# Two-layer hybrid decoder trunk on one core: gate/up columns in another order, the FFN's input at 64-byte multiples, and narrow passes at the start of two stretches

## The chip, the cores and the metric

The kernel runs on one core of a Trainium2 chip. The metric is device time in microseconds (us) of one execution. TensorE (PE in the profile, with PEld for its weight loads) multiplies, VectorE (DVE) and ScalarE (ACT) do the elementwise work, SyncE (SP) issues the transfers, GpSimd (POOL) does next to nothing here.

## The reference

Two layers over 256 positions and 1024 features. In each layer a SwiGLU feed-forward block (FFN), a mixer (low-rank attention beside a short convolution) and a second FFN; each starts from an RMS norm whose output is scaled and shifted by values computed from a conditioning vector.

```python
for l in range(DEPTH):
    mod = jnp.split(c_act @ w_ada[l] + b_ada[l], N_MOD, axis=-1)
    h = modulate(rms_norm(x, ffn1_norm[l]), mod[0], mod[1])
    x = x + FFN_RESIDUAL * (1 + mod[2])[:, None, :] * swiglu(h, ffn1_w_gu[l], ffn1_w_down[l])
    h = modulate(rms_norm(x, mix_norm[l]), mod[3], mod[4])
    y = hybrid_mixer(h, cos, sin, w_in[l], ...)
    x = x + (1 + mod[5])[:, None, :] * y
    h = modulate(rms_norm(x, ffn2_norm[l]), mod[6], mod[7])
    x = x + FFN_RESIDUAL * (1 + mod[8])[:, None, :] * swiglu(h, ffn2_w_gu[l], ffn2_w_down[l])
return rms_norm(x, final_norm)
# swiglu(h, w_gu, w_down): g, u = split(h @ w_gu); (silu(g) * u) @ w_down     with D_FF = 2816
```

## The kernel before

Features lie on the 128 partitions: `x` is 8 rows of 128 features by 256 positions, and so is the FFN's input `u`. Every weight is read from memory once, in chunks of 16 tiles of 128 by 128 (1 MB).

**Precision by parts.** A float32 factor is split into a rounded high part and the remainder. ACT makes `hi` of a chunk and DVE makes `lo` from `raw` and `hi` (L262 and L265), two halves of eight tiles each; ACT and DVE do the same for the input, into uH (L355) and uL (L359, L361). A weight tile then takes the products hi·uH, hi·uL and lo·uH. In `mm3` these are three passes of 256 columns. In `mm3w` ("wide") one pass of 512 columns takes uL and uH together, since they lie side by side, and a second pass of 256 columns adds lo·uH. With `split`, `mm3w` issues the 512 columns as two passes of 256 ("narrow"). Each pass loads its weights anew.

**The FFN.** There are four, here named by layer and place: (0,0), (0,2), (1,0), (1,2). Each has 22 gate/up chunks: chunk j holds the eight tiles (over the eight input rows k) of 128 gate columns and the eight of 128 up columns, in the order k = 0 gate, k = 0 up, k = 1 gate, and so on. The output of a chunk goes through ACT and DVE (Silu, product, split) into the tile `a`, a row of 2048 bytes for each chunk. Then come 11 down chunks: for each of eight output blocks m, 22 tiles, each fed by one row of `a`.

The first four chunks of (0,2), (1,0) and (1,2) ("late", `LATE = 4`) run on an unnormed input, in narrow passes with two more columns for the shift, while the norm is still being computed; their results are corrected afterwards. During the fourth one ACT and DVE write the normed and modulated input into `u`, row by row (the L355 and L359 instructions that read `qh` and `e`). From the fifth chunk on (j = 4) the passes are wide and read `u`. FFN (0,0) runs its gate/up in narrow passes throughout.

**The layout of u.** One tile with rows of 2·256 + 2 = 514 float32, that is 2056 bytes, which is 32 times 64 plus 8: row k begins 8k bytes past a multiple of 64. The first 256 columns are uL, then uH, then the shift's two columns.

**Order.** PE, DVE and ACT each work through one queue in order. The order in it is made by a list scheduler from priorities: `due` sets them, from a clock that each matmul advances by its columns, with leads for loads and slack for evacuations. The mixer's order on PE and SP is written by hand, and so is SP's throughout: for each chunk the load of `raw` and, behind it, the loads of `ada` (w_ada, from which DVE computes the modulation at L189). `raw`, `hi` and `lo` have three buffers each, `ada` four.

The split passes before: one whole chunk, (1,0) j = 21, and in the down part the first 4 tiles of (0,2) and the first 22 of (1,2):

```python
mm3w(pt[:, h, :], w, 2 * k + h, u[:, k, :2 * S], uH[:, k, :S], k == 0, k == KD - 1, (l, sub, j) == (1, 0, NJ - 1))
...
mm3w(ps, w, t % 16, aB[k], aH[k], k == 0, k == NJ - 1, t < (0 if sub == 0 else 22 if l else 4))
```

Of the kernel before, what the change touches and what calls it, by code (L numbers as in the profile page):

```python
# [12 lines left out]
F32R = mybir.dt.float32r  # L13
# [5 lines left out]
P = 128  # L19
L = 2  # L20
D = 1024
S = 256
KD = D // P
FF = 2816
NJ = FF // P
# [6 lines left out]
CH = 16 * P  # L32
# [3 lines left out]
LATE = 4  # L36
# [2 lines left out]
ENGS = {'p': mybir.EngineType.PE, 's': mybir.EngineType.SP, 'v': mybir.EngineType.DVE, 'a': mybir.EngineType.Activation}  # L39
MAN = 'sp'  # L40
SM_ACT = 2
ORDER = ("K K Q Q K X K Q Q P P P L c c c P c N Z V v q0 q1 s0 q2 c c c c t0 s1 a0 q3 c c c t1 c a1 s2 s3 c c c c t2 d d a2 t3 d a3 "
         "d d n d w d d A A A w m A A w A A A B B B B B B B B").split()
WIN = dict(K=0, Q=1, P=2, c=3, d=7)
# [75 lines left out]
def trunk(ctx: ExitStack, tc, x_d, c_d, pos_d, small_d, cst_d, ada_d, gu1_d, dn1_d, win_d, up_d, wo_d, gu2_d, dn2_d, out_d):  # L120
    nc = tc.nc
    one = ctx.enter_context(tc.tile_pool(name="one", bufs=1))
# [7 lines left out]
    def nm(s):  # L130
        uid[0] += 1
        return f"{s}_{uid[0]}"
# [7 lines left out]
    def work(shape, tag, bufs=2, dt=F32):  # L140
        return wk.tile(shape, dt, tag=tag, name=nm(tag), bufs=bufs)
# [4 lines left out]
    x = one.tile([P, KD, S], F32, name="x")  # L146
    cb = one.tile([P, D], F32, name="cb")
    small = one.tile([P, SM_W], F32, name="small")
    cst = one.tile([P, C_W], F32, name="cst")
    u = one.tile([P, KD, 2 * S + 2], F32R, name="u")  # L150
    uL, uH = u[:, :, 0:S], u[:, :, S:]
    ones = one.tile([P, P], F32, name="ones")
    tq = one.tile([P, S], F32, name="tq")
    tk = one.tile([P, S], F32, name="tk")
# [135 lines left out]
    def mm3(dst, w, t, aH, aL, first, last, ext=0):  # L290
        hi, lo = w[-2:]
        n = S + ext
        wh = hi[:, t * P:(t + 1) * P]
        wl = lo[:, t * P:(t + 1) * P]
        mm(dst[:, :n], wh, aH[:, :n], start=first, stop=False, skip_group_check=True)
        mm(dst[:, :S], wh, aL, start=False, stop=False, skip_group_check=True)
        mm(dst[:, :n], wl, aH[:, :n], start=False, stop=last, skip_group_check=True)

    def mm3w(dst, w, t, both, up, first, last, split=False):


        hi, lo = w[-2:]
        wh = hi[:, t * P:(t + 1) * P]
        wl = lo[:, t * P:(t + 1) * P]
        if split:
            mm(dst[:, :S], wh, both[:, :S], start=first, stop=False, skip_group_check=True)
            mm(dst[:, S:], wh, both[:, S:], start=False, stop=False, skip_group_check=True)
        else:
            mm(dst, wh, both, start=first, stop=False, skip_group_check=True)
        mm(dst[:, :S], wl, up, start=False, stop=last, skip_group_check=True)  # L310
# [43 lines left out]
    def hi_of(dH, src, scale=1.0):  # L354
        nc.scalar.activation(dH, src, AF.Copy, scale=scale)  # L355

    def lo_of(dL, dH, src, scale=None):
        if scale is None:
            nc.vector.tensor_tensor(dL, src, f32(dH), ALU.subtract)  # L359
        else:  # L360
            nc.vector.scalar_tensor_tensor(dL, src, scale, f32(dH), ALU.mult, ALU.subtract)  # L361

    class Pre:


        def __init__(self, l, sub):
            self.l, self.sub = l, sub
            self.gs = work([P, 8], "gs", 2)
            self.stat = Stat(D)

# [7 lines left out]
            return g  # L378

        def shifts(self):  # L380
            hcol = uH[:, :, S:S + 1].squeeze(2)
            lcol = uH[:, :, S + 1:S + 2].squeeze(2)
            sh = self.shift(0, KD)
            nc.scalar.activation(hcol, sh, AF.Copy)
            nc.vector.tensor_tensor(lcol, sh, f32(hcol), ALU.subtract)

        def put(self, k, add=True):
            g = self.scale(k)
            hi_of(uH[:, k, :S], x[:, k, :], g)
            lo_of(uL[:, k, :], uH[:, k, :S], x[:, k, :], g)  # L390
            if add:
                self.stat.add(x[:, k, :])

# [15 lines left out]
    def ffn(l, sub, pre, nxt, first=False):  # L409
        def evac(j, pg, pu, r):  # L410
# [20 lines left out]
            if j == NJ - 1:  # L431
                warm(sg[:, 0:1], AF.Abs_reciprocal_sqrt)

        j0 = 0
        if first:
            r = work([P, S], "r", 1)
# [12 lines left out]
            with tc.manual_schedule():  # L449
# [18 lines left out]
                for k in range(KD):  # L468
# [6 lines left out]
                    w, top, rest = load(True) if k else w0  # L475
# [22 lines left out]
        aL, aH = ([ab[k // (NJ // 2)][:, k % (NJ // 2), q, :] for k in range(NJ)] for q in range(2))  # L498
        aB = [ab[k // (NJ // 2)][:, k % (NJ // 2)].rearrange("p a s -> p (a s)") for k in range(NJ)]
        for j in range(j0):  # L500
            z = slice((j % 2) * S, (j % 2 + 1) * S)
            due(GU_SLACK + 1000 * j)
            evac(j, pts[j // 2][:, 0, z], pts[j // 2][:, 1, z], None)
        for j in range(j0, NJ):
            w = chunk()
            if first and j == 10:
                due(ROPE_SLACK)
                nc.sync.dma_start(cst, cst_d)
                nc.sync.dma_start(pi, pos_d)
                rope()  # L510
            late = not first and j < LATE
            wide = not first and not late
            pt = ps_tile()
            for k in range(KD):
                for h in range(2):
                    if wide:
                        mm3w(pt[:, h, :], w, 2 * k + h, u[:, k, :2 * S], uH[:, k, :S], k == 0, k == KD - 1, (l, sub, j) == (1, 0, NJ - 1))
                    else:
                        mm3(pt[:, h, :], w, 2 * k + h, uH[:, k, :], uL[:, k, :], k == 0, k == KD - 1, 2 if late else 0)
            if late and j == 0:  # L520
                r = work([P, S], "r", 1)
                pre.stat.rstd(r, then=AF.Silu)
                due(0)
                hs = [work([P, 2, S], "qh", 2) for _ in range(2)]
                he = [work([P, 2, 384], "e", 2).rearrange("p a b -> p (a b)") for _ in range(2)]
                hf = [hs[k // 2][:, k % 2, :] if k < 4 else he[k // 2 - 2][:, k % 2 * S:(k % 2 + 1) * S] for k in range(KD)]
                for k in range(KD):
                    xr = work([P, S], "nt", 2)
                    nc.vector.tensor_tensor(xr, x[:, k, :], r, ALU.mult)  # L529
                    nc.scalar.activation(hf[k], xr, AF.Identity, scale=pre.gs[:, k:k + 1], bias=pre.shift(k))  # L530
            if late and j == LATE - 1:
                due(-URGENT)
                for k in range(KD):
                    hi_of(uH[:, k, :S], hf[k])
                    lo_of(uL[:, k, :], uH[:, k, :S], hf[k])
            due(GU_SLACK if j < NJ - 3 else 0)
            if late:
                evac(j, pt, None, r)
            elif wide:
                evac(j, pt, None, None)  # L540
            else:
                evac(j, pt[:, 0, :S], pt[:, 1, :S], None)
        if nxt is None:
            y = [wk.tile([P, 4, S], F32, tag="ada", name=nm("y"), bufs=4) for _ in range(2)]
        for t in range(KD * NJ):
            m, k = divmod(t, NJ)
            if t % 16 == 0:
                w = chunk()
            if k == 0:
                ps = ps_tile()[:, 0, :]  # L550
            if m < KD - 1:
                mm3w(ps, w, t % 16, aB[k], aH[k], k == 0, k == NJ - 1, t < (0 if sub == 0 else 22 if l else 4))
            else:
                mm3(ps, w, t % 16, aH[k], aL[k], k == 0, k == NJ - 1)
            if k == NJ - 1:
                due(DN_SLACK if m < KD - 1 else -URGENT)
                residual(ps, m, l, sub, 0.5, m < KD - 1)
                if nxt is None:
                    if m == KD - 1:
                        psf = ps_tile()[:, 0, :S]  # L560
                        fin.sums(psf, True, False)
                        due(-URGENT)
                        fin.acc = None
                    fin.add(x[:, m, :])
                    nc.scalar.activation(y[m // 4][:, m % 4, :], x[:, m, :], AF.Copy, scale=small[:, L * SM_L + m:L * SM_L + m + 1])
                    if m == KD - 1:
                        last_norm(psf, y)
                else:
                    nxt.put(m)
                    if m == 5:  # L570
                        nxt.shifts()

    def mixer(l, pre, nxt):
        mf = one.tile([P, NJ, S], F32, tag="aH", name=nm("mf"))
        mr = one.tile([P, NJ, S], F32R, tag="aL", name=nm("mr"))
        ckv, cq, conv, V, K = mf[:, 0:2], mf[:, 2:5], mf[:, 5:9], mf[:, 9:13], mf[:, 13:21]
# [317 lines left out]
    pre = Pre(0, 0)  # L894
# [18 lines left out]
def _layout(a):  # L913
    g = {}
# [17 lines left out]
    for f in (1, 2):  # L932
        t = _tiles(a[f"ffn{f}_w_gu"]).reshape(L, KD, 2, NJ, P, P)
        w = t.transpose(0, 3, 4, 1, 2, 5).reshape(L, NJ, P, CH)
        if f == 1:
            head = w[0, :8].reshape(8, P, 8, 2, P).transpose(2, 1, 0, 3, 4).reshape(1, 8, P, CH)
            w = np.concatenate([np.concatenate([head, w[:1, 8:]], axis=1), w[1:]], axis=0)
        g[f"gu{f}"] = np.ascontiguousarray(w)
        t = _tiles(a[f"ffn{f}_w_down"]).transpose(0, 2, 1, 3, 4).reshape(L, 11, 16, P, P)
        g[f"dn{f}"] = np.ascontiguousarray(t.transpose(0, 1, 3, 2, 4).reshape(L, 11, P, CH))  # L940
    w = a["w_in"]
# [41 lines left out]
```

## Time and profile before

| | |
|---|---|
| three runs | 993.0, 990.76, 993.14 us, median 993.0 |
| profiled execution | 993.62 us, of which 990.9 us are the span of its instructions |
| granted TensorE clock | 0.998 |
| DVE, ACT busy | 852.4 us (86%), 580.3 us (59%) |
| read from memory | 248.59 MB, 252 GB/s over the span |

The page gives for each engine how long it was busy, then the chain of work that ended last, then groups of instructions. The records of matmuls overlap, because they are pipelined: a pass of 512 columns is recorded with 0.39 us and the next one starts some 0.23 us after it began. How fast the passes follow each other is therefore read from starts, or from the number of passes in a stretch, and not from their mean duration. Which stretch is which, in us from the start of the span: FFN (0,0) to 205, mixer to 311, (0,2) gate/up to 438 and down to 500, (1,0) gate/up from there to 627 and down to 689, mixer to 794, (1,2) gate/up to 919 and down to the end.

### The profile page before, as it was taken

How to read it: one execution, taken by the hardware profiler on the slowest of the kernel's cores; microseconds unless marked ns; L12 is line 12 of the kernel's file. 1: busy time of each engine (PE TensorE's matmuls, PEld its weight loads, DVE VectorE, ACT ScalarE, POOL GpSimd, SP SyncE). 2: the span in 40 equal slices, each digit the busy share in tenths (PEclk: the TensorE clock that was granted, in tenths of full speed). 3: DMA queues.
4: the chain of work that ended last, by engine and by line, in shares of the span. 5: the costliest groups of instructions: out<-in, count | busy, mean ns of one | idle time of the engine just before them, and what ended most of it. 6: DMA issues, size and time to landing. Idle time of an engine off the chain costs nothing.

```text
span 990.9 us, 16909 instructions
## 1 busy us (share of the span) xinstructions
PE 973.8 (98%) x6602; PEld 897.2 (91%) x6602; DVE 852.4 (86%) x1598; ACT 580.3 (59%) x1010; POOL 8.0 (1%) x27
## 2 busy tenths in 40 slices
PE   8999999999999999999999999999999999999996
PEld 7999998899999988888898888889999998888985
DVE  5999999999989999888879988888899999866653
ACT  4474544468758756554466555544687676556551
POOL 0000020000000000000000000000000000000000
PEclk9999999999999999999999999999999999999999
DMA  9999898873746688777867877876455467555531
GB/s 348 382 361 349 321 327 322 298 306 137 263 161 239 216 323 327 272 267 271 292 217 294 291 282 260 304 273 247 149 211 195 149 240 294 210 184 198 176 123 42
DMA packets 47007, 250.78 MB, mean 253 GB/s; under 512 B 5504, under 2 KB 5824, under 8 KB 26576
## 3 DMA queue, kind: packets, MB, share of 16 engines
q1 hardware_dynamic: 46224, 248.81, 68.5%
q8 instruction: 51, 0.84, 0.3%
q10 hardware_dynamic: 288, 0.65, 0.2%
q0 software_dynamic: 416, 0.25, 0.1%
q14 instruction: 28, 0.23, 0.1%
HBM read 248.59 MB, written 1.10 MB: 252 GB/s over the span
## 4 chain that ended last, share of the span: by engine, by line
PE 88%; DVE 6%; DMA 3%; ACT 1%; issue 1%; DVEq 0%; SPq 0%; ACTq 0%
PE ps L287 87%; DVE lo L265 2%; DMA raw<-in_gu 2%; DMA ada<-in_ada 1%; DVE ada L189 1%; PE ps L736 1%; ACT hi L262 1%; DMA cb<-in_c 0%; DVE acc L326 0%; DVE u L361 0%; DVE x L399 0%; DVE nt L599 0%; DVE mr L359 0%; DVE nt L529 0%; DVE rs_a L347 0%
## 5 line engine op out<-in xcount | busy, mean ns | idle before, releaser
L287 PE MATMUL ps<-u,hi 128*128 128x256 f32 (+2 forms) x2480 | 596.6, 322 | 2.6 <-DVE u L359 1.1
L287 PE MATMUL ps<-u,lo 128*128 128x256 f32 (+1 forms) x1664 | 469.1, 282 | 1.1 <-DVE lo L265 1.1
L287 PEld LDWEIGHTS ps<-u,hi 128*128 128x128 f32 x2480 | 413.1, 189 | 40.9 <-ACT hi L262 1.3
L265 DVE TENSOR_TENSOR lo<-raw,hi 128x1024 fp32r<-128x1024 f32 (+2 forms) x384 | 394.5, 1045 | 38.3 <-ACT hi L262 38.0
L262 ACT ACTIVATE hi<-raw 128x1024 fp32r<-128x1024 f32 (+2 forms) x384 | 336.9, 911 | 91.3 <-PE ps L287 37.3
L287 PEld LDWEIGHTS ps<-u,lo 128*128 128x128 f32 x1664 | 314.7, 189 | 1.6 <-DVE lo L265 1.6
L287 PE MATMUL ps<-a,hi 128*128 128x512 f32 (+1 forms) x818 | 247.9, 364 | 0.0
L189 DVE CUSTOM_DVE_ANT_0 ada<-ada,cb,small 128x1024 f32<-128x1024 f32 x144 | 183.0, 1279 | 32.7 <-DMA ada<-in_ada 32.6
L287 PE MATMUL ps<-a,lo 128*128 128x256 f32 x704 | 197.8, 281 | 0.0
L287 PEld LDWEIGHTS ps<-a,hi 128*128 128x128 f32 x818 | 145.9, 188 | 26.2 <-DVE a L359 0.2
L287 PEld LDWEIGHTS ps<-a,lo 128*128 128x128 f32 x704 | 133.2, 189 | 0.0
L355 ACT ACTIVATE a<-cc 128x256 fp32r<-128x256 f32 x88 | 36.3, 415 | 63.0 <-DVE cc L418 54.0
L287 PE MATMUL ps<-mr,hi 128*128 128x256 f32 x384 | 71.3, 286 | 0.7 <-ACT mr L355 0.5
L355 ACT ACTIVATE u<-x,gs 128x256 fp32r<-128x256 f32 x40 | 19.9, 506 | 80.4 <-DVE x L399 80.1
L287 PEld LDWEIGHTS ps<-mr,hi 128*128 128x128 f32 x384 | 60.3, 191 | 2.2 <-ACT mr L355 0.9
L287 PE MATMUL ps<-mr,lo 128*128 128x256 f32 x192 | 54.7, 285 | 0.0
L399 DVE SCALAR_TENSOR_TENSOR x<-ps,gate,x 128x256 f32<-128x256 f32 x76 | 36.0, 480 | 17.7 <-PE ps L287 17.1
L417 ACT ACTIVATE cc<-g 128x256 f32<-128x256 f32 x54 | 22.5, 417 | 45.3 <-DVE g L416 45.2
L359 DVE TENSOR_TENSOR a<-cc,a 128x256 fp32r<-128x256 f32 x88 | 36.7, 420 | 12.6 <-ACT a L355 12.5
L287 PEld LDWEIGHTS ps<-mr,lo 128*128 128x128 f32 x192 | 36.7, 191 | 0.8 <-DVE lo L265 0.8
L416 DVE TENSOR_TENSOR g<-ps,g 128x512 f32<-128x512 f32 x54 | 36.9, 684 | 0.4 <-ACT g L415 0.4
L415 ACT ACTIVATE g<-ps 128x512 f32<-128x512 f32 x54 | 31.3, 579 | 7.7 <-PE ps L287 7.7
(121 smaller groups left out, 566.1 us busy)
## 6 DMA issues: line engine op xcount, KB each, us to landing
raw<-in_gu SPq DMA_DIRECT2D x87, 1024.0 KB, 5.8
ada<-in_ada SPq DMA_DIRECT2D x144, 512.0 KB, 6.2
raw<-in_dn SPq DMA_DIRECT2D x44, 1024.0 KB, 5.2
raw<-in_win SPq DMA_DIRECT2D x18, 1024.0 KB, 5.0
raw<-in_wo SPq DMA_DIRECT2D x8, 1024.0 KB, 4.9
raw<-in_up SPq DMA_DIRECT2D x2, 1024.0 KB, 5.5
raw<-in_up SPq DMA_DIRECT2D x2, 768.0 KB, 5.0
raw<-in_up SPq DMA_DIRECT2D x4, 384.0 KB, 3.2
```

The source lines that it names most:

```text
L189: nc.vector.tensor_tensor_reduce(out=a, in0=a, in1=cb, scale=1.0, scalar=sm(l, t), op0=ALU.mult, op1=ALU.add, accum_out=mods[l][:, t:t + 1])
L262: nc.scalar.activation(hi[:, zs[q]], raw[:, zs[q]], AF.Copy)
L265: nc.vector.tensor_tensor(lo[:, zs[q]], raw[:, zs[q]], f32(hi[:, zs[q]]), ALU.subtract)
L287: nc.tensor.matmul(dst, a, b, **kw)
L355: nc.scalar.activation(dH, src, AF.Copy, scale=scale)
L359: nc.vector.tensor_tensor(dL, src, f32(dH), ALU.subtract)
L399: nc.vector.scalar_tensor_tensor(x[:, m, :], s, g, x[:, m, :], ALU.mult, ALU.add)
L415: nc.scalar.activation(t2, pg[:, :, :S], AF.Copy)
L416: nc.vector.tensor_tensor(t2, pg[:, :, S:], t2, ALU.add)
L417: nc.scalar.activation(sg, t2[:, 0, :], AF.Silu)
L736: nc.tensor.transpose(ps[:, e, z], d["e"][:, e, z], ident)
```

## The change

- From the fifth chunk on, in (0,2), (1,0) and (1,2), a chunk holds its eight gate tiles first and its eight up tiles after them, and the loop runs so (`h` outside, `k` inside). The weights are laid out accordingly beforehand, so the 16 tiles of a chunk are still read front to back.
- `u` becomes a flat tile `uf` with two views on the same bytes: `u_near` with the old rows of 2056 bytes, for (0,0) and the mixers, and `u_far` with rows of 528 float32 or 2112 bytes, 33 times 64, for (0,2), (1,0) and (1,2).
- Narrow passes: the whole chunk j = 4 in these three FFNs (before: j = 21 of (1,0)), and the whole first output block of the down part, 22 tiles, in these three (before: 4, 0 and 22 tiles).

```diff
+U_NEAR, U_FAR, U_COLS = 0, 0, 2 * S + 16
...
-    u = one.tile([P, KD, 2 * S + 2], F32R, name="u")
-    uL, uH = u[:, :, 0:S], u[:, :, S:]
+    uf = one.tile([P, U_FAR + KD * U_COLS], F32R, name="u")
+    u_far = uf[:, U_FAR:].rearrange("p (k c) -> p k c", c=U_COLS)[:, :, :2 * S + 2]
+    u_near = uf[:, U_NEAR:U_NEAR + KD * (2 * S + 2)].rearrange("p (k c) -> p k c", c=2 * S + 2)
...
+            self.u = u_near if sub == 1 or (l, sub) == (0, 0) else u_far
+            self.uL, self.uH = self.u[:, :, 0:S], self.u[:, :, S:]
...
-            for k in range(KD):
+            for h in range(2 * wide):
+                for k in range(KD):
+                    mm3w(pt[:, h, :], w, h * KD + k, u[:, k, :2 * S], uH[:, k, :S], k == 0, k == KD - 1, j == LATE)
+            for k in range(KD * (not wide)):
                 for h in range(2):
-                    if wide:
-                        mm3w(pt[:, h, :], w, 2 * k + h, u[:, k, :2 * S], uH[:, k, :S], k == 0, k == KD - 1, (l, sub, j) == (1, 0, NJ - 1))
-                    else:
-                        mm3(pt[:, h, :], w, 2 * k + h, uH[:, k, :], uL[:, k, :], k == 0, k == KD - 1, 2 if late else 0)
+                    mm3(pt[:, h, :], w, 2 * k + h, uH[:, k, :], uL[:, k, :], k == 0, k == KD - 1, 2 if late else 0)
...
-                mm3w(ps, w, t % 16, aB[k], aH[k], k == 0, k == NJ - 1, t < (0 if sub == 0 else 22 if l else 4))
+                mm3w(ps, w, t % 16, aB[k], aH[k], k == 0, k == NJ - 1, m == 0 and (l, sub) != (0, 0))
...
+        for q in range(2 - f, L):
+            z = w[q, LATE:].reshape(NJ - LATE, P, KD, 2, P)
+            w[q, LATE:] = z.swapaxes(2, 3).reshape(NJ - LATE, P, CH)
```

The same place on PE, before: the last pass of the late chunks of FFN (1,0) and the first tiles of j = 4, with what each pass waits for (hi and lo are the weights, ps the accumulator).

```order
L287 MATMUL ps_5827<-u,lo_5818 128x258
L287 MATMUL ps_5912<-u,hi_5902 128x512 [waits DVE_49]
L287 MATMUL ps_5912<-u,lo_5903 128x256
L287 MATMUL ps_5912<-u,hi_5902 128x512
L287 MATMUL ps_5912<-u,lo_5903 128x256
L287 MATMUL ps_5912<-u,hi_5902 128x512 [waits DVE_49]
L287 MATMUL ps_5912<-u,lo_5903 128x256
L287 MATMUL ps_5912<-u,hi_5902 128x512
L287 MATMUL ps_5912<-u,lo_5903 128x256
L287 MATMUL ps_5912<-u,hi_5902 128x512 [waits DVE_49]
```

And there after the change:

```order
L289 MATMUL ps_5861<-u,lo_5852 128x258
L289 MATMUL ps_5946<-u,hi_5936 128x256 [waits DVE_49]
L289 MATMUL ps_5946<-u,hi_5936 128x256 [waits Activation_49]
L289 MATMUL ps_5946<-u,lo_5937 128x256
L289 MATMUL ps_5946<-u,hi_5936 128x256 [waits DVE_49]
L289 MATMUL ps_5946<-u,hi_5936 128x256 [waits Activation_49]
L289 MATMUL ps_5946<-u,lo_5937 128x256
L289 MATMUL ps_5946<-u,hi_5936 128x256 [waits DVE_49]
L289 MATMUL ps_5946<-u,hi_5936 128x256 [waits Activation_49]
L289 MATMUL ps_5946<-u,lo_5937 128x256
```

Before, every second tile waits for a new row of u (two tiles share a row); now every tile does, until the eight rows are through, and a tile has three passes.

The other side of these waits, DVE in the same place, before: it writes the low part of the eight rows (u from qh, then from e; the first row's instruction stands just ahead of this piece), between other work: cc, a, gb and g belong to the evacuation of chunks, lo is a half of a weight chunk.

```order
L428 SCALAR_TENSOR_TENSOR cc_5807<-g_746_5810,gb_5808,cc_5807 128x256 [waits Activation_49]
L359 TENSOR_TENSOR u<-qh_5641,u 128x256 [waits Activation_49]
L359 TENSOR_TENSOR u<-qh_5642,u 128x256 [waits Activation_49]
L359 TENSOR_TENSOR a_5566<-cc_5807,a_5566 128x256 [waits Activation_49]
L359 TENSOR_TENSOR u<-qh_5642,u 128x256 [waits Activation_49]
L359 TENSOR_TENSOR u<-e_5643,u 128x256 [waits Activation_49]
L265 TENSOR_TENSOR lo_5955<-raw_5953,hi_5954 128x1024 [waits DMAHW6_49]
L359 TENSOR_TENSOR u<-e_5643,u 128x256 [waits Activation_49]
L359 TENSOR_TENSOR u<-e_5644,u 128x256 [waits Activation_49]
L424 TENSOR_REDUCE gb_5893<-ps_5827 128x2 [waits PE_49]
L426 TENSOR_TENSOR g_754_5895<-ps_5827,r_5628 128x512
L359 TENSOR_TENSOR u<-e_5644,u 128x256 [waits Activation_49]
```

And there after the change:

```order
L432 SCALAR_TENSOR_TENSOR cc_5841<-g_746_5844,gb_5842,cc_5841 128x256 [waits Activation_49]
L361 TENSOR_TENSOR u<-qh_5675,u 128x256 [waits Activation_49]
L361 TENSOR_TENSOR u<-qh_5676,u 128x256 [waits Activation_49]
L361 TENSOR_TENSOR a_5600<-cc_5841,a_5600 128x256 [waits Activation_49]
L361 TENSOR_TENSOR u<-qh_5676,u 128x256 [waits Activation_49]
L361 TENSOR_TENSOR u<-e_5677,u 128x256 [waits Activation_49]
L267 TENSOR_TENSOR lo_6005<-raw_6003,hi_6004 128x1024 [waits DMAHW6_49]
L361 TENSOR_TENSOR u<-e_5677,u 128x256 [waits Activation_49]
L361 TENSOR_TENSOR u<-e_5678,u 128x256 [waits Activation_49]
L428 TENSOR_REDUCE gb_5927<-ps_5861 128x2 [waits PE_49]
L430 TENSOR_TENSOR g_754_5929<-ps_5861,r_5662 128x512
L361 TENSOR_TENSOR u<-e_5678,u 128x256 [waits Activation_49]
```

Nothing moved here: only the numbers of lines and buffers differ. SP and POOL keep their order throughout. Elsewhere DVE and ACT exchange some neighbours, and the instruction that writes the shift's column into u stands later in two FFNs, behind the rows written before it.

More of the change, by code (lines that the diff above doesn't have):

```diff
@@ L380, in shifts @@
         def shifts(self):
-            hcol = uH[:, :, S:S + 1].squeeze(2)
-            lcol = uH[:, :, S + 1:S + 2].squeeze(2)
+            hcol = self.uH[:, :, S:S + 1].squeeze(2)
+            lcol = self.uH[:, :, S + 1:S + 2].squeeze(2)
             sh = self.shift(0, KD)
@@ L388, in put @@
             g = self.scale(k)
-            hi_of(uH[:, k, :S], x[:, k, :], g)
-            lo_of(uL[:, k, :], uH[:, k, :S], x[:, k, :], g)
+            hi_of(self.uH[:, k, :S], x[:, k, :], g)
+            lo_of(self.uL[:, k, :], self.uH[:, k, :S], x[:, k, :], g)
             if add:
@@ L432, in evac @@
                 warm(sg[:, 0:1], AF.Abs_reciprocal_sqrt)
+        u, uL, uH = pre.u, pre.uL, pre.uH
         j0 = 0
@@ L573, in mixer @@
     def mixer(l, pre, nxt):
+        uL, uH = pre.uL, pre.uH
         mf = one.tile([P, NJ, S], F32, tag="aH", name=nm("mf"))
@@ L937, in _layout @@
             w = np.concatenate([np.concatenate([head, w[:1, 8:]], axis=1), w[1:]], axis=0)
-        g[f"gu{f}"] = np.ascontiguousarray(w)
+        w = np.ascontiguousarray(w)
+        for q in range(2 - f, L):
+            z = w[q, LATE:].reshape(NJ - LATE, P, KD, 2, P)
+            w[q, LATE:] = z.swapaxes(2, 3).reshape(NJ - LATE, P, CH)
+        g[f"gu{f}"] = w
         t = _tiles(a[f"ffn{f}_w_down"]).transpose(0, 2, 1, 3, 4).reshape(L, 11, 16, P, P)
```

## The prediction

> **What bounds the kernel now.** I read the page first: span, busy shares, the chain that ended last.
>
> ```profile
> span 990.9 us, 16909 instructions
> PE 88%; DVE 6%; DMA 3%; ACT 1%; issue 1%; DVEq 0%; SPq 0%; ACTq 0%
> ```
>
> PE carries 88% of the chain, so the time is the number of passes times their spacing, plus a few waits. The next question is the spacing. Below are PE's records in stretches without a wait: three of gate/up, then down of (0,0), (0,2), (1,0), (1,2), then late chunks of (1,0).
>
> ```profile
> core 0: us, PE busy (x), PEclk, DMA share, GB/s
> 345.00:435.00 90.00, 90.00 (x515) 1.00 0.82 298
> 535.00:618.00 83.00, 83.00 (x475) 1.00 0.81 295
> 825.00:915.00 90.00, 90.00 (x515) 1.00 0.63 222
> 146.00:196.00 50.00, 50.00 (x290) 1.00 0.87 323
> 442.00:491.50 49.50, 49.50 (x281) 1.00 0.76 275
> 636.00:681.00 45.00, 45.00 (x256) 1.00 0.73 259
> 928.00:972.00 44.00, 44.00 (x256) 1.00 0.35 120
> 508.60:525.20 16.60, 16.60 (x140) 1.00 0.53 192
> ```
>
> About two passes are in progress at any instant, so a stretch holds x − 2 starts, and a wide tile is two passes. Gate/up: 90/256.5 = 0.351 us a tile in all three. Down: 50/144 = 0.347, 49.5/139.5 = 0.355, 45/127 = 0.354, 44/127 = 0.346. The same tile has **two spacings in the down part**, and neither follows the transfers: the first has the most traffic (323 GB/s), the last the least, and both are fast. Single starts sharpen it: three tiles of (0,0), three of (0,2).
>
> ```profile
> 159.82 0.39 PE L287 MATMUL ps<-a,hi 128*128 128x512 f32 x1
> ...
> 160.86 0.39 PE L287 MATMUL ps<-a,hi 128*128 128x512 f32 x1
> 459.85 0.40 PE L287 MATMUL ps<-a,hi 128*128 128x512 f32 x1
> ...
> 460.91 0.40 PE L287 MATMUL ps<-a,hi 128*128 128x512 f32 x1
> ```
>
> 1.04/3 = 0.3467 and 1.06/3 = 0.3533. I call them the fast and the slow rhythm; each holds for a whole stretch. Input rows in down lie at multiples of 64 bytes; in gate/up they don't, and the spacing is between the two. Fast were the stretch that follows narrow gate/up, (0,0), and the one with 22 narrow tiles ahead, (1,2). Slow were 4 narrow tiles ahead, (0,2), and none ahead, (1,0). That is four cases for a rule, no proof.
>
> **Gate/up spacing.** The edit makes gate/up's input like down's: rows at multiples of 64 bytes, sixteen passes after each other into one accumulator. If it takes the fast rhythm, a wide tile drops from 0.351 to 0.3467. A narrow tile is three passes: by the last row of the table 16.6/138 = 0.120 us each, 0.360. Per FFN after: 16 × 0.360 + 272 × 0.3467 = 100.06. Before, 288 × 0.351 = 101.09 in (0,2) and (1,2), and 272 × 0.351 + 16 × 0.360 = 101.23 in (1,0). So −1.03, −1.17 and −1.03. Bounds: the slow rhythm on one side (272 × 0.3533 + 5.76 = 101.86: +0.77, +0.63, +0.77), the fast one on the other. I take the fast one: each such stretch now follows 48 narrow passes, and in down the long narrow start went with it.
>
> **Down spacing.** (0,2): 4 × 0.360 + 150 × 0.3533 = 54.44 becomes 22 × 0.360 + 132 × 0.3467 = 53.68, −0.76. (1,0): 154 × 0.3533 = 54.41 becomes 53.68, −0.73. (1,2) has its 22 already, 0; (0,0) isn't touched. At the other bound +0.12, +0.15 and, if (1,2) lost its rhythm, +0.88.
>
> In all 72 wide passes become two. At 0.360 − 0.3467 = 0.0133 us each that costs 0.96 us, which the sums above contain. The Trainium skill (TensorE: Matmul & The Clock Gate, "Wait — 56ns, not 53.3ns?") gives a fixed cost of about 2.5 ns to a warm pass; by it the 72 would cost an estimated 0.2 us. The rows above disagree, at 0.120 us for 256 columns, and I use the rows.
>
> **The new waits.** In j = 4 PE now needs all eight rows of u within eight tiles, 2.9 us, where it had sixteen, 5.6 us. What is queued behind a waiting pass is all of PE. DVE's order is unchanged, so its times of before tell when the rows come. First (1,0):
>
> ```profile
> 525.57 0.49 PE L287 MATMUL ps<-u,hi 128*128 128x512 f32 x1
> 525.09 0.41 DVE L359 TENSOR_TENSOR u<-qh,u 128x256 fp32r<-128x256 f32 x1
> 525.82 0.75 DVE L359 TENSOR_TENSOR u<-qh,u 128x256 fp32r<-128x256 f32 x2
> 526.83 0.41 DVE L359 TENSOR_TENSOR u<-qh,u 128x256 fp32r<-128x256 f32 x1
> 527.17 0.41 DVE L359 TENSOR_TENSOR u<-e,u 128x256 fp32r<-128x256 f32 x1
> 527.50 1.21 DVE L265 TENSOR_TENSOR lo<-raw,hi 128x1024 fp32r<-128x1024 f32 x1
> 528.64 0.75 DVE L359 TENSOR_TENSOR u<-e,u 128x256 fp32r<-128x256 f32 x2
> 529.38 0.68 DVE L426 TENSOR_TENSOR g<-ps,r 128x512 f32<-128x512 f32 x1
> 529.98 0.41 DVE L359 TENSOR_TENSOR u<-e,u 128x256 fp32r<-128x256 f32 x1
> ```
>
> The eighth row is ready at 530.39; PE starts about 0.07 later (525.50 to 525.57 for the first) and is through the gate tiles at 530.46 + 0.36 = 530.8. Without waits it would be 525.57 + 8 × 0.36 = 528.45. So **+2.3 us**, because one half of lo and one g stand between the rows. Bounds: 0, if DVE came there earlier than before against PE, and 2.4. I take 2.3, since DVE is busy without a gap in these rows. In (0,2) and (1,2):
>
> ```profile
> 336.81 0.47 PE L287 MATMUL ps<-u,hi 128*128 128x512 f32 x1 [1.09 <-DVE u L359]
> 337.59 1.42 DVE L359 TENSOR_TENSOR u<-e,u 128x256 fp32r<-128x256 f32 x4
> 818.02 0.39 PE L287 MATMUL ps<-u,hi 128*128 128x512 f32 x1
> 819.79 0.41 DVE L359 TENSOR_TENSOR u<-e,u 128x256 fp32r<-128x256 f32 x1
> ```
>
> The eighth row is ready at 339.01 and needed at 336.81 + 7 × 0.36 = 339.33; at 820.20 and needed at 820.54. Cost 0, with 0.3 us of cover; without it, as much as DVE is late.
>
> **What a faster PE runs into.** The pieces of the chain at the end of (0,2):
>
> ```profile
> 492.94 2.28 DVE lo L265 x2
> 495.62 7.86 DMA ada<-in_ada
> 503.50 1.28 DVE ada L189
> 505.49 1.22 DVE lo L265
> 507.17 225.81 PE ps L287 x1461
> 447.10 1.23 DVE L265 TENSOR_TENSOR lo<-raw,hi 128x1024 fp32r<-128x1024 f32 x1 [0.64 <-ACT hi L262]
> ```
>
> The last residual and u rows of (0,2) stand on DVE behind an ada product that waits 7.86 us for its transfer; SP issued that behind a raw load, which waited for DVE's lo to free a buffer. That loop doesn't contain PE, and PE waits at its end. So the 1.03 + 0.76 = 1.79 us gained in (0,2) mostly lengthen that wait. What may pass is the 0.64 us that DVE stood at 447.10 for ACT's hi (if ACT waited there for a weight buffer that PE frees): I count −0.6, bounds 0 and −1.79. From 507.17 to 733 the chain is PE alone, so the gains of (1,0) count. In (1,2) DVE has slack:
>
> ```profile
> 858.49 1.23 DVE L265 TENSOR_TENSOR lo<-raw,hi 128x1024 fp32r<-128x1024 f32 x1 [1.41 <-ACT hi L262]
> ```
>
> The moved writes of the shift's columns cost nothing: they are still in the down part, ahead of the late chunks that read them; their cover is that part, tens of us.
>
> **Sum:** −0.6 + 2.3 − 1.17 − 0.73 − 1.03 = −1.2 us. The profiled execution took 993.62 (2.7 us outside its span), which gives 992.4; it lies 0.6 above the median of 993.0, and I forecast the median: **991.8 us**. A measurement here tells about 0.3%, 3 us, from no change.
>
> **Rivals.**
> 1. All gains arrive and the rows of u come in time: −1.03 − 1.17 − 1.03 − 0.76 − 0.73 = −4.7, 988.3 us. For it: ada's transfer time may differ from run to run (the three runs differ by 2.4 us), and both losses I count are waits, not work. Against it: DVE's order there is unchanged and without gaps.
> 2. The slow rhythm. The aligned inputs settle as in the down parts of (0,2) and (1,0): 0.3533 a tile. (0,2)'s +0.9 hides in the wait at 505; (1,0) +0.63 + 0.15, (1,2) +0.77 + 0.88, the wait +2.3: **+4.7, 997.7 us**. It decides from the point where the 544 wide tiles of (1,0) and (1,2) lose the forecast's 1.2 us again, 2.2 ns of the 4.3 that each gains, that is at a spacing above 0.349. For it: two of four aligned stretches are slow. Against it: neither had a long narrow start on aligned rows.
> 3. The alignment does nothing. Gate/up stays at 0.351, the narrow chunk costs 16 × 0.009 = 0.14 in (0,2) (hidden) and (1,2), nothing in (1,0), down of (1,0) gains 0.73, the wait stays: +0.14 − 0.73 + 2.3 = +1.7, 994.7 us. For it: the mean spacing of gate/up is that of the four aligned stretches, 0.350.
>
> **How the numbers follow.** Forecast 0.48, of which 0.04 lie more than 3 us below; rival 1 0.20; rival 2 0.18, of which 0.02 within 3 us, if only some stretches are slow; rival 3 0.14, of which 0.02 above. Faster 0.24, same 0.58, slower 0.18. The range leaves out the lower half of rival 1 (0.10) and the upper half of rival 2 (0.09): 988.4 to 996.8 us. The forecast's own range, with −1.79 to 0 for (0,2) and 2.3 to 2.4 for the wait, is 990.6 to 992.5.
>
> **What would show it.** In stretches of gate/up the count of records over the same 90 us tells the rhythm: 521 for fast, 511 for slow, 515 for no change. Down of (0,2) and (1,0) should count like (1,2). In j = 4 of (1,0) PE should show waits for u of about 2.3 us in all, and none in the other two. The wait at the end of (0,2) should grow by more than 1 us. The forecast is wrong if gate/up isn't at 0.347, or if (1,0) shows no such waits.

## The result and the profile after

The changed kernel takes 999.03 us (median of four, 996.93 to 1000.2) against 992.14 (990.76 to 993.14) for the kernel before: ratio **1.0061, 95% interval 1.0039 to 1.0083**. It is slower by 0.6%; the forecast was 991.8, with a range up to 996.8. The profiled execution took 997.9 us, of which 996.1 are its span. The page, span and chain:

```profile
span 996.1 us, 17044 instructions
PE 77%; DVE 13%; DMA 7%; ACT 2%; issue 1%; SPq 0%; DVEq 0%; ACTq 0%
```

PE has lost 11 points of the chain, and DVE and DMA have them. So the time went to waits. PE's records by stretch, answering to the windows of before (start and end in us, then PE busy and passes, granted clock, share of the DMA engines, GB/s); three of gate/up, the first down block of (0,2), then down of (0,2), (1,0) and (1,2):

```profile
345.00:435.00 90.00, 90.00 (x517) 1.00 0.82 298
541.00:624.00 83.00, 83.00 (x478) 1.00 0.80 292
830.00:920.00 90.00, 90.00 (x517) 1.00 0.64 225
447.80:451.00 3.20, 3.13 (x12) 0.59 0.78 253
452.00:494.50 42.50, 42.50 (x248) 1.00 0.73 266
641.00:685.50 44.50, 44.50 (x254) 1.00 0.72 258
933.00:977.00 44.00, 44.00 (x251) 1.00 0.35 120
```

Gate/up got a little quicker: 517 passes where there were 515 and the forecast had 521. By single starts a tile takes 0.3492 us, before 0.3508. Down of (0,2) is now in the quick rhythm (42.5/123 = 0.346), (1,0) is unchanged (44.5/126 = 0.353), and (1,2) has fallen into the long one: 251 passes in 44 us where there were 256. And there is a window at a clock of 0.59, which the kernel before doesn't show. Where PE stands in time, from the starts of its passes:

| place | before | after | later by |
|---|---|---|---|
| (0,2): first down tile | 437.93 | 438.17 | 0.24 |
| (0,2): last down pass | 500.15 | 503.44 | **3.29** |
| (1,0): last late pass | 525.45 | 529.46 | 4.01 |
| (1,0): first down tile | 626.88 | 631.30 | 4.42 |
| (1,0): last down pass | 689.27 | 693.66 | 4.39 |
| (1,2): first down tile | 919.06 | 923.38 | 4.32 |
| (1,2): last down pass | 980.53 | 985.73 | **5.20** |

The largest step lies in the down part of (0,2). PE there, after the change (start, duration, instruction, in brackets its idle time and who ended it):

```profile
445.60 0.28 PE L289 MATMUL ps<-a,lo 128*128 128x256 f32 x1
447.87 0.50 PE L289 MATMUL ps<-a,hi 128*128 128x256 f32 x2 [1.99 <-DVE a L361]
448.21 0.28 PE L289 MATMUL ps<-a,lo 128*128 128x256 f32 x1
448.33 0.56 PE L289 MATMUL ps<-a,hi 128*128 128x512 f32 x1
448.69 0.41 PE L289 MATMUL ps<-a,lo 128*128 128x256 f32 x1
448.90 0.63 PE L289 MATMUL ps<-a,hi 128*128 128x512 f32 x1
```

PE stands 2.27 us from start to start, where 0.12 are usual, for the last row of `a`. Then five wide tiles take 0.64 us each (448.90 to 449.54 is one of them) instead of 0.347, since the clock was lowered: 5 × 0.293 = 1.5 us more. Wait and clock are 2.15 + 1.5 = 3.6 us. The rest of this down part gave 0.6 back, by 18 more narrow tiles (+0.24) and the other rhythm (132 × 0.0067 = −0.88).

Why was `a` late? DVE in the last chunk before, from the end of chunk j = 20 on (lines left out are marked):

```profile
439.31 0.42 DVE L359 TENSOR_TENSOR a<-cc,a 128x256 fp32r<-128x256 f32 x1 [0.40 <-ACT a L355]
439.65 1.27 DVE L189 CUSTOM_DVE_ANT_0 ada<-ada,cb,small 128x1024 f32<-128x1024 f32 x1
...
440.86 1.22 DVE L265 TENSOR_TENSOR lo<-raw,hi 128x1024 fp32r<-128x1024 f32 x1
442.00 0.68 DVE L416 TENSOR_TENSOR g<-ps,g 128x512 f32<-128x512 f32 x1
...
444.63 0.42 DVE L359 TENSOR_TENSOR a<-cc,a 128x256 fp32r<-128x256 f32 x1 [0.48 <-ACT a L355]
```

and after:

```profile
441.98 0.42 DVE L361 TENSOR_TENSOR a<-cc,a 128x256 fp32r<-128x256 f32 x1 [0.40 <-ACT a L357]
442.98 1.28 DVE L191 CUSTOM_DVE_ANT_0 ada<-ada,cb,small 128x1024 f32<-128x1024 f32 x1 [0.57 <-DMA ada<-in_ada]
...
444.19 0.68 DVE L420 TENSOR_TENSOR g<-ps,g 128x512 f32<-128x512 f32 x1
444.80 1.21 DVE L267 TENSOR_TENSOR lo<-raw,hi 128x1024 fp32r<-128x1024 f32 x1
...
447.40 0.41 DVE L361 TENSOR_TENSOR a<-cc,a 128x256 fp32r<-128x256 f32 x1
```

Before, the last `a` ends at 445.05, and the tile that reads it, the 22nd, is due at 437.93 + 4 × 0.36 + 17 × 0.353 = 445.37. **The margin was 0.3 us.** After, `a` ends at 447.8. Neighbours have changed places: g now stands ahead of the first half of lo, directly behind the ada product, and cc ahead of the second half. Further back in this stretch every second chunk has this new order. In both orders g, cc and lo stand behind the ada product and wait with it when its transfer is late. The chain of waits after the change shows a loop:

```profile
419.13 1.28 DVE ada L191
...
424.07 8.16 DMA ada<-in_ada
...
432.25 1.29 DVE ada L191
...
433.55 0.60 DVE g L420
434.15 1.13 DVE lo L267
435.28 0.35 DVE cc L422
...
435.98 1.05 ACT hi L264
437.03 0.11 SPq L254
...
437.19 5.77 DMA ada<-in_ada
...
442.98 1.28 DVE ada L191
...
444.27 0.60 DVE g L420
```

One link of it the chain names wrongly: SP's raw load doesn't wait for ACT's hi, which ends only after that load has begun. It begins right after the second half of lo, which frees its buffer. First after the change, then before it:

```profile
435.54 1.22 DVE L267 TENSOR_TENSOR lo<-raw,hi 128x1024 fp32r<-128x1024 f32 x1
436.82 0.33 SPq L254 DMA_DIRECT2D raw<-in_dn  x1
437.19 0.43 SPq L182 DMA_DIRECT2D ada<-in_ada  x1
434.33 1.28 DVE L189 CUSTOM_DVE_ANT_0 ada<-ada,cb,small 128x1024 f32<-128x1024 f32 x1
...
437.28 1.22 DVE L265 TENSOR_TENSOR lo<-raw,hi 128x1024 fp32r<-128x1024 f32 x1
438.52 0.33 SPq L252 DMA_DIRECT2D raw<-in_dn  x1
438.89 0.43 SPq L180 DMA_DIRECT2D ada<-in_ada  x1
```

So SP issues the ada load behind a raw load, which waits for DVE's lo, and lo stands behind an ada product. One turn serves two chunks and takes the transfer plus about 5 us: 432.25 − 419.13 = 13.1 us, then 442.98 − 432.25 = 10.7. PE needs 2 × 16 × 0.349 = 11.2. In the new order the load is issued 4.94 us after the ada product starts (432.25 to 437.19), in the old one 4.56 (434.33 to 438.89), since cc now stands ahead of the second half of lo. So a transfer may take 6.2 us without a wait in the new order and 6.6 in the old. The 19 loads of ada in this stretch after the change took 3.6 to 8.5 us from issue to landing, half of them over 6.0. Whether DVE keeps up depends on how long each takes. That the new order makes DVE late is theory Q below.

### The profile page after: what moved, and what is told of

It reads as the page before. It is cut to its first block, busy times and chain, and to the rows that moved or that the text cites. A ratio compares the mean times of both kernels' runs of the same rounds, so it can differ in the third digit from the quotient of the medians.

```text
span 996.1 us, 17044 instructions
## 1 busy us (share of the span) xinstructions
PE 975.7 (98%) x6674; PEld 901.7 (91%) x6674; DVE 852.7 (86%) x1598; ACT 581.0 (58%) x1010; POOL 8.0 (1%) x27
## 4 chain that ended last, share of the span: by engine, by line
PE 77%; DVE 13%; DMA 7%; ACT 2%; issue 1%; SPq 0%; DVEq 0%; ACTq 0%
PE ps L289 76%; DVE lo L267 4%; DMA ada<-in_ada 3%; DMA raw<-in_gu 3%; DVE ada L191 2%; ACT hi L264 1%; DVE g L420 1%; PE ps L742 1%; DVE nt L534 1%; DMA cb<-in_c 0%; DVE acc L328 0%; DVE a L361 0%; DVE u L363 0%; DVE x L403 0%; DVE cc L422 0%
## 5 line engine op out<-in xcount | busy, mean ns | idle before, releaser
L289 PE MATMUL ps<-u,hi 128*128 128x258 f32 (+2 forms) x2512 | 596.2, 320 | 4.0 <-DVE u L361 1.7
L289 PEld LDWEIGHTS ps<-a,hi 128*128 128x128 f32 x858 | 151.8, 190 | 26.7 <-DVE a L361 2.2
L361 DVE TENSOR_TENSOR a<-cc,a 128x256 fp32r<-128x256 f32 x88 | 36.8, 421 | 10.8 <-ACT a L357 10.7
```

What stands on the lines that cost most here:

```text
L289: nc.tensor.matmul(dst, a, b, **kw)
```

## The experiments

Every kernel ran beside the kernel before on the same chip. The executions of both scatter, and the scatter is part of the finding: those of the kernel before by 2.4 us in the four above and by 6 to 13 us in the sets of 19 to 31 below. So besides ratio and interval I give how many executions were above 994.5 us.

**The parts.** Four kernels on one chip, before there 991.33 us (4 of 31 above 994.5). The narrow chunk alone:

```diff
-... (l, sub, j) == (1, 0, NJ - 1))
+... j == LATE)
```

> The kernel before, with the narrow chunk moved from j = 21 of (1,0) to j = 4 of the three later FFNs, and nothing else of the change. Theory Q (queue): the narrow chunk makes the scheduler put ada's product ahead of g and cc on DVE in gate/up of (0,2); DVE then stands there for ada's transfer, the outputs of the last chunk come late, PE waits about 2 us in the first down block of (0,2) and its clock drops after that. By Q this kernel alone is 3 to 6 us slower than before, with a wait of PE over 1.5 us between 440 and 450 and a granted clock under 0.9 behind it. Theory R (rows and rhythm): the loss comes from the rows of u that are needed twice as fast and from the slow rhythm; by R this kernel is within 1 us of before (32 more passes at 0.0133 us less 0.2), without such a wait.

Measured: 991.72, ratio 1.0001 (0.9979 to 1.0023), 2 of 10 above 994.5. Its profiled execution (995.07 us) shows the wait of theory Q, 445.69 to 447.90, with the lowered clock behind it; the median shows nothing of it, though theory Q expected 3 to 6 us.

The whole change with the old narrow chunk instead of j = 4:

> The whole change except the narrow chunk, which stays at j = 21 of (1,0): rows of 2112 bytes, eight gate tiles then eight up tiles, 22 narrow tiles at the start of the down parts. Theory Q: DVE's order is that of before, no wait at the start of down in (0,2), gate/up at 0.349 us a tile (as in the changed kernel), a wait of 1 to 2 us for rows in (1,0), so 990 to 993 us. Theory R: the loss stays, 996 to 999 us.

991.35, ratio 0.9995 (0.9977 to 1.0012), none of 10 above 994.5. At the 22nd tile of (0,2) PE waits under 0.5 us. Gate/up is at 0.3492, down of (0,2) in the quick rhythm, (1,0) and (1,2) in the long one. Theory R, by which the loss would stay, falls.

Only the 22 narrow down tiles:

```diff
-... t < (0 if sub == 0 else 22 if l else 4))
+... m == 0 and (l, sub) != (0, 0))
```

> The kernel before, with 22 narrow tiles at the start of the down parts of (0,2), (1,0) and (1,2) instead of 4, 0 and 22. If the long narrow start decides the rhythm: 0.3467 us a tile in all four down parts, 1.5 us less than before. If it doesn't (in the changed kernel (1,0) and (1,2) were slow in spite of it): 0.3533 in at least one, and a time within 1 us of before. Q and R alike expect no wait at the start of down in (0,2).

990.76, ratio 0.9990 (0.9965 to 1.0015), 1 of 10; the profile fell on that one (998.25): PE stands 3.87 us at the 22nd down tile of (1,0). The down parts of (0,2) and (1,2) are in the quick rhythm and that of (1,0) is in the long one, all with 22 narrow tiles.

Only the rows of 2112 bytes:

> The kernel before, with rows of 2112 bytes for u in the three later FFNs and nothing else. If the rows set gate/up's spacing: 0.349 us a tile in all three, 1.5 us less than before, by 848 tiles times 1.8 ns. If the order of the tiles (sixteen passes into one accumulator after each other, each row of u read again after eight tiles) sets it: 0.351, and the time of before.

994.03, ratio 1.0026 (1.0002 to 1.0051), 5 of 10. PE stands 2.62 us at the 22nd down tile of (1,0). Gate/up is at 0.3500: alignment alone brings half of what the change brings there, and the 1.5 us that 0.349 would have saved didn't come.

No part alone loses the 0.6%, and each profile in which PE lost time shows the same wait at the 22nd down tile, in (0,2) or in (1,0).

**The order on DVE.** The next four on another chip, where before took 994.26 (15 of 31 above 994.5). The changed kernel again:

> The changed kernel itself, for how often it is disturbed beside the two halves of the change. Theory Q (the narrow chunk j = 4 makes the scheduler set ada ahead of g, cc and a on DVE at the end of (0,2)'s gate/up; DVE waits for ada's transfer there, is late at the start of down, PE stands over 2 us for a and its clock drops): most executions 995 to 1000, with mean clocks of 0.993 to 0.996, and a gap of 2 us or more near 446. Rival A (the first measurement met a bad chip): median 991 to 993, like the two halves alone.

997.5, ratio 1.0048 (1.0023 to 1.0074), **10 of 10** above 994.5. The loss holds on a second chip. This profile shows three waits: 1.2 us at 446 in (0,2), 2.07 us at 506 at the end of (0,2), and one in (1,0), here with PE's rows and the window behind them:

```profile
637.22 0.28 PE L289 MATMUL ps<-a,lo 128*128 128x256 f32 x1
641.35 0.79 PE L289 MATMUL ps<-a,hi 128*128 128x256 f32 x2 [3.85 <-DVE a L361]
641.30:643.90 2.60, 2.55 (x9) 0.50 0.73 280
```

With j = 4 narrow in its first two tiles alone (`j == LATE and h == 0 and k < 2`), which leaves DVE the old order of ada and g:

> The whole change, but in j = 4 only the first two gate tiles are narrow. DVE's order in (0,2) is then that of the kernel before. Theory Q: no PE gap over 1 us near 446, clock 0.997 to 0.998, median 989.5 to 992. Rival R (the loss is the change's spacings and rhythms, which two or sixteen narrow tiles do not alter): median 996 or more, like the changed kernel.

994.48, ratio 0.9993 (0.9969 to 1.0016), 4 of 10. The absolute time missed what I wrote, because that chip took 994 for the kernel before too; against that kernel the loss is gone. PE still waits 1.6 us at the 22nd tile of (0,2), without a lowered clock.

The whole change with each ada load issued a chunk earlier, and the kernel before with the same:

```diff
             nc.sync.dma_start(raw[:, :n], src)
+            if 49 <= i < 115:
+                ada_load(ada_target(i + 2))
             due(lead[1])
```

> The whole change, and SP issues each ada load of the chunks from (0,2) to (1,0) one chunk earlier, so that DVE's product finds it there. Theory Q: no wait of DVE for ada's transfer over 0.5 us between 420 and 447, no PE gap over 1 us near 446 and near 634, clock 0.998, median 988 to 991. Rival T (memory traffic is the limit in (0,2), so that a transfer issued earlier comes no earlier, or delays raw): DVE then waits for raw or hi as long, PE stands over 2 us near 446, median 995 or more.

> The kernel before, with the ada loads one chunk earlier as in e7. Theory Q: its late executions of 994 to 998 (about a quarter of them) go, median 989 to 991 and highest under 993. Rival T: no difference, or slower, with the same spread.

e7: 992.88, ratio 1.0005 (0.9975 to 1.0034), 3 of 10. e8: 992.43, ratio 0.9987 (0.9965 to 1.0008), 2 of 10. On the same chip the changed kernel had 997.5 and 10 of 10 (e5); with all its work done and only the loads earlier, it is 0.45 us behind e8, though the intervals of e5 and e7 still overlap a little. Both medians stay above the 988 to 991 that were expected, and e8 still has executions of 995 and 997. In (0,2) the last `a` now comes 5.4 us after the first down tile in both, 2 us ahead of its need. In (1,0) the waits for ada are no shorter than before (9.6 and 8.8 us against 7.0), so some late executions remain. Theory Q holds for (0,2), not for (1,0).

**Is the order enough?** Before on the third chip: 993.62 (7 of 19). One priority of the kernel before is moved, which gives DVE the changed order in (0,2) and changes nothing on PE:

```diff
-            due(lead[1])
+            due(lead[1] + (-600 if 56 <= i < 57 else 0))
```

> The kernel before with one ada product's priority moved by 600 (chunk j = 7 of (0,2)), which gives DVE at the end of (0,2)'s gate/up the order of the changed kernel (ada ahead of g and lo) and leaves PE's work as it was. Theory Q alone: DVE is late at the start of (0,2)'s down as in the changed kernel, median 3 to 6 us above that of the kernel before, PE gap of 1.2 to 2.3 us near 446. Rival M (the order costs only together with something else of the change, since the narrow chunk alone has this order too and lost nothing in the median): median within 2 us of the kernel before.

993.55, ratio 1.0012 (0.9986 to 1.0039), 5 of 10, up to 1000.5. **Theory Q alone falls:** the order alone isn't the loss. What it does shows in a table over the profiles. The columns "idle for ada" are DVE's idle time ahead of its ada products, from 101 us before the first down tile to 12 after it; the columns "last `a`" the end of the last `a` after the first down tile. PE needs it 7.4 to 7.6 us after that tile.

| kernel | (0,2): idle for ada | (0,2): last `a` | (1,0): idle for ada | (1,0): last `a` |
|---|---|---|---|---|
| before | 3.4 | 7.1 | 7.0 | 7.4 |
| e2, e3, e4, e6, e12 (old order) | 4.1, 2.8, 2.4, 4.5, 2.4 | 7.9, 7.1, 6.7, 9.0, 6.2 | 6.5, 10.7, 9.3, 7.5, 12.7 | 5.8, 11.3, 9.9, 6.6, 11.3 |
| after, e5 | 7.3, 6.4 | 9.6, 8.6 | 4.0, 12.3 | 6.1, 11.5 |
| e1, e9, e10, e15, e16 (new order) | 6.9, 5.9, 6.2, 5.2, 6.1 | 9.5, 7.0, 8.3, 7.6, 8.4 | 7.7, 7.4, 9.7, 9.9, 11.7 | 6.2, 7.5, 7.3, 6.9, 10.8 |
| e7, e8, e11 (ada earlier) | 1.5, 0.7, 1.7 | 5.4, 5.4, 5.4 | 9.6, 8.8, 5.8 | 8.7, 7.4, 5.4 |
| e17, e18 (ada moved) | 0.7, 2.3 | 5.3, 6.3 | 0.4, 0.0 | 6.3, 5.3 |

The order doubles DVE's wait for ada in (0,2), without overlap: 2.4 to 4.5 in the old one, 5.2 to 7.3 in the new. In (1,0) every second chunk has ada directly ahead of g in the kernel before too, and the wait differs by 8 us between two executions of the same kernel (after and e5). What PE loses at the 22nd tile is the last `a` minus 7.5, and nothing below that: a threshold. The new theory, L: the loss is DVE's loop through ada's transfer, wherever it closes, and PE pays what exceeds the margin.

It also closes at a place that the table leaves out, the end of (0,2), where the last rows of u stand behind the ada products of the down part. From the last down pass of (0,2) to the last late pass of (1,0) PE takes 23.3 to 23.5 us in ten of the 20 profiles (e1, e2, e7 to e9, e12 to e14, e17, e18) and 24.3 to 28.9 in the others: 25.3 before, 26.0 after, 28.9 in e15. So the kernel before pays there too, and how much is a draw.

Beside e9 ran three others. The change with rows of 2176 bytes (`U_COLS = 2 * S + 32`):

> The whole change with rows of u at 2176 bytes, 34 times 64, instead of 2112, 33 times 64. If the remaining spread of gate/up's tiles comes from where a row begins within a larger block of memory, the cycle over the eight rows (344 to 357 ns) becomes a shorter one of four and the mean of 0.3492 moves towards 0.3467. If it comes from the stops between accumulators, the cycle stays and the mean is 0.349.

One execution, 996.58. The cycle over the rows became one of two tiles, 348 and 352 ns by the starts, and the mean is 0.3500. So the row's place sets the cycle, but neither pitch tried brought 0.3467.

The change without the narrow chunk and with ada a chunk earlier:

> The change without the narrow chunk j = 4 (j = 21 of (1,0) narrow as before), with the ada loads one chunk earlier. Theory Q: no PE gap over 1.3 us near 446 and 634; gate/up 0.349; median 1 to 3 us below that of the kernel before and a narrower spread. If the ada wait was not what made the late executions, the spread is that of the kernel before.

992.85, ratio 0.9987 (0.9968 to 1.0006), 1 of 10 above 994.5. Fewer late executions, but not clearly below the kernel before. The profile fell on the late one (995.66): PE waits for nothing at the 22nd tiles, but loses 2.2 us at the end of (0,2) and 2.6 at the rows of u in (1,0).

Only gate tiles first, then up tiles:

> Only the order within a chunk (eight gate tiles, then eight up tiles), old rows and old narrow passes; DVE's order is that of the kernel before. If the rows' alignment is what moved gate/up from 0.351 to 0.349, the spacing here stays at 0.351 and down of (1,2) stays fast (0.3467). If the order of the tiles did half of it, 0.350.

One execution, 995.08; gate/up at 0.3500, so the order of the tiles gives the other half. PE stands 4.09 us at the 22nd down tile of (1,0). Down of (1,2) is in the long rhythm.

**All of it?** The fourth chip, before 995.01 (16 of 28). Both kernels without 39 of ada's 144 loads and products, most of those in the two gate/up parts, so that their results differ:

```diff
+            if 66 <= len(ada_tiles) < 84 or 97 <= len(ada_tiles) < 118:
+                ada_tiles.append(None)
+                continue
             a = wk.tile([P, D], F32, tag="ada", name=nm("ada"), bufs=4)
...
+            if a is None:
+                continue
```

> The changed kernel without the ada products and their loads in the gate/up parts of (0,2) and (1,0) (39 of 144; their modulation columns are zero, so the result differs). Theory L (the loss is DVE's loop through ada's transfer; the rest of the change is worth less than 1 us): no PE gap over 1.3 us near 446 and 634, clock 0.998, all executions within 2 us, and within 1 us of e14. Rival: the loss of 5 us against e14 stays, so it lies in PE's spacings or elsewhere.

> The kernel before without the same ada products and loads. Theory L: its late executions (995 and more) go too, median 987 to 990, all within 2 us. It is the base for e13.

e13: 990.37 (988.99 to 990.66). e14: 989.73 (989.05 to 989.86). Both are free of the scatter, and **the changed kernel is 0.6 us behind, not 5 or 6**. Theory L holds. These two runs also take DVE work and traffic away; e7 against e5 and e8, where all work is done, is what points to the wait for the transfer.

The two narrow parts together, and the whole change without the rows of 2112 bytes:

> The narrow chunk j = 4 and the narrow first down block together, old rows and old order within a chunk. Theory M (DVE's new order costs about 3 us of waits for ada in (0,2), and how much of it PE meets depends on the rest): between the narrow chunk alone (ratio 1.000) and the whole change (1.005), 1.002 to 1.004. If the rows and the chunk's order are needed for the loss: 1.000.

> The whole change without the rows of 2112 bytes. Theory M: 1.003 to 1.005, since DVE's order and PE's work at the start of down are those of the changed kernel. If the rows are needed for the loss: 1.000 to 1.002.

e15: 996.06, ratio 1.0009 (0.9982 to 1.0036), 6 of 10; its profile has a wait of 2.88 us at the end of (0,2), with the lowered clock behind it. e16: 997.69, ratio 1.0037 (1.0008 to 1.0066), 8 of 10; PE stands 3.47 us at the 22nd down tile of (1,0). Against e1 (1.0001) and the whole (1.0048 and 1.0061) the loss grows with each part that is added, but neighbouring intervals overlap and the runs are from several chips, e1 from the least disturbed: how much each part adds stays open.

Last, all of ada's work, spread otherwise, on the chip where before is least disturbed (992.06, 1 of 19):

```diff
-PACE = ... (33, 58), (49, 64), (84, 97), (117, 130), ...
+PACE = ... (33, 58), (49, 70), (71, 82), (82, 100), (104, 110), (115, 128), (117, 130), ...
```

> The kernel before with the same ada products spread otherwise: 12 instead of 20 in the gate/up part of (0,2) and 10 instead of 20 in that of (1,0), the rest in the mixer ahead and in the two down parts, where DVE has room. Theory L: no PE gap over 1.3 us near 446 and 634, executions of 995 and more become rare, median 990 to 992 and 2 us or more below that of the kernel before where that is disturbed often. Rival: the products in the mixer or the down parts delay residuals or norms, and the time moves there: median 993 or more.

> The changed kernel with the same spread of ada. Theory L: median within 1 us of e17 (0.6 us above, as e13 against e14), so the loss of the change is gone while all its work is done. Rival: 3 us or more above e17.

e17: 992.29 (991.51 to 992.91), ratio 0.9998 (0.9987 to 1.0009). e18: 992.64 (992.04 to 993.08), ratio 1.0004 (0.9992 to 1.0016). None of 20 executions is above 994.5, and the change costs 0.35 us. The changed kernel with the old spread wasn't run on this chip, so these two runs show that no loss is there, but not by themselves that the new spread removed it. The 2 us of gain were expected where the kernel before is disturbed often, so that stays untested, and 992.29 lies just above the 990 to 992. By the end of the first mixer PE is 3.6 us later than in the profile before, 0.9 of it from ahead of the mixer, with a new wait of 1.5 us at 289 and two of about 0.5 at 232, which is the rival; the way from there to the end of (1,0)'s gate/up then gives 3.3 of that back (the first down tile of (1,0) is 0.34 later). The same spread without more ada in the mixer wasn't tried. No kernel here that does all the work is clearly below the kernel before.

## Why the prediction was wrong

**The step that failed** is the one on what runs beside PE: "Elsewhere DVE and ACT exchange some neighbours" was in the change, and its price in the sum was nothing. Also "DVE's order is unchanged" was true only for the rows of u. The loop through ada's transfer was in the prediction, with the right links, but at one place, the end of (0,2), as a cover that swallows gains. The sum has one length of the transfer, and rival 1 let it differ only as a gain. It is a loop that runs through all of (0,2)'s and (1,0)'s gate/up, with a turn of 10.7 to 13.1 us against PE's 11.2, and it ends at a tile with 0.3 us of margin. That margin could be read in the profile before, from the last `a` (445.05) against the tile that needs it (445.37). The narrow chunk j = 4 was charged with waits for u. What it mainly did was to change the scheduler's order from a few chunks behind it to the end of the stretch, some 15 chunks later.

The terms on PE can now be read apart from that, in e17 against e18, neither of which waits at the two places. PE's windows of e17 (gate/up of the three FFNs, then down of (1,2)):

```profile
348.00:438.00 90.00, 90.00 (x515) 1.00 0.77 284
536.00:619.00 83.00, 83.00 (x475) 1.00 0.72 258
826.00:916.00 90.00, 90.00 (x515) 1.00 0.64 223
929.00:969.00 40.00, 40.00 (x232) 1.00 0.38 132
```

and of e18:

```profile
348.00:438.00 90.00, 90.00 (x517) 1.00 0.77 282
536.00:619.00 83.00, 83.00 (x478) 1.00 0.72 261
826.00:916.00 90.00, 90.00 (x517) 1.00 0.63 219
929.00:969.00 40.00, 40.00 (x228) 1.00 0.37 130
```

| term, (0,2) / (1,0) / (1,2) | forecast | e18 − e17 |
|---|---|---|
| gate/up, last late pass to first down tile | −1.03 / −1.17 (+2.3 of waits) / −1.03 | −0.36 / −0.49 / −0.38 |
| down | −0.76 / −0.73 / 0 | +0.13 / +0.14 / +0.88 |

- **Gate/up at 0.3467** was the wrong value of a right direction: 0.3492, two fifths of the gain. The rows' place alone (0.3500) and the tiles' order alone (0.3500) did half of it each.
- **Down's rhythm** came out at the bounds that the text gave, +0.12, +0.15 and +0.88, not at the value taken. (In the first profile after the change (0,2) alone was quick, as forecast.) "The long narrow start" isn't what sets it: all of these kernels have 22 narrow tiles at the start of (1,2)'s down part, and its rhythm was long in the 12 profiles with changed rows or tile order in gate/up and quick in the 8 without. Rival 2 had that part right; its 997.7 us came near the result by another mechanism.
- **The waits for u** in (1,0) were 0.9 us, not 2.3, and none in e18. PE came 4.0 us later than before and DVE with the eighth row only 2.6 (532.99 against 530.39), which is the difference of 1.4. The 11 profiles with the gate tiles first have 0 to 2.6 us here (2.3 in e16), so this term is a draw as well. Two waits of 0.34 and 0.52 above the usual 0.12 remain, behind the half of lo and the g that the text named:

```profile
531.24 0.28 PE L289 MATMUL ps<-u,lo 128*128 128x256 f32 x1
531.70 0.51 PE L289 MATMUL ps<-u,hi 128*128 128x256 f32 x2 [0.18 <-DVE u L361]
532.40 0.28 PE L289 MATMUL ps<-u,lo 128*128 128x256 f32 x1
533.04 0.50 PE L289 MATMUL ps<-u,hi 128*128 128x256 f32 x2 [0.36 <-DVE u L361]
```

- **The wait at the end of (0,2)** should grow by over 1 us; in the profile after it grew by 0.8 (PE's starts at 508.44 and 510.06, before 505.16 and 505.98), and its size is a draw.

Without the loop the change is worth −0.1 us by these terms (their sum), and +0.35 and +0.6 by the medians of e17, e18 and of e13, e14. The forecast of −1.2 was 1.1 to 1.8 us off there. The other 4 to 6 us of the measured loss are the waits of the loop and the clock behind them.

## What to carry to other kernels

A reordering by the scheduler is part of the change, even where it is far away: compare the order on every engine, and price each swapped pair by what is queued behind the one that can wait for a transfer. Look for loops through a transfer, add up a turn, and compare it with the same stretch of PE; where the two are close, a result of one profile is one draw of a scatter. At the places where one stage starts on the last product of another, read the margin in the profile before; 0.3 us is a threshold, not a cover.

## What the runs showed of the hardware

- **A short wait lowers the clock.** After each of the eight PE gaps of 2.21 to 4.13 us from start to start (2.21, 2.27, 2.62, 2.88, 3.47, 3.87, 4.09, 4.13) the granted clock was 0.50 for 3.41 us, after the one of 3.87 (e3) for 6.83 us, and a wide tile took 0.64 us. After gaps of 1.2, 1.63 and 2.07 us it stayed at 1.00. So in these profiles a wait beyond about 2.1 us costs some 1.5 us more, and 2.4 in e3. The Trainium skill (TensorE: Matmul & The Clock Gate, "What's actually happening") puts the fall to half clock after an idle window of about 3.4 us; the runs show it after less. The Trainium skill (the same page, "Wait — 56ns, not 53.3ns?") spaces passes at half clock by columns over 1.2 GHz, an estimated 640 ns for 512 + 256; the measured 0.64 us agrees.
- **One tile, several spacings.** The same two passes follow each other in 0.3467 or 0.3534 us in down, and in cycles over the rows in gate/up: eight tiles of 344 to 358 ns at rows of 2112 bytes, two of 348 and 352 at 2176. Which rhythm (1,2)'s down part takes was the same in all profiles with the same gate/up ahead of it. In (1,0) it differs between two executions of the changed kernel (0.3534 in the first profile, 0.3467 in e5), so the program alone doesn't decide it; what does is open.
